# FFN heads of a four-layer fp32 trunk: one weight sum moved ahead of a side's low half, and down weights split behind the last gate

## Chip, core and metric

The kernel runs on one core of a Trainium2 chip. The metric is device time in microseconds (us), the median of several runs. Five engines work side by side, each through its own instructions in order: TensorE (PE in the profile; PEld is its loading of stationary operands), VectorE (DVE), ScalarE (ACT), GpSimd (POOL) and SyncE (SP). SP and POOL issue the DMA transfers here, each in the order of its queue.

## What is computed

A trunk of four layers on a sequence of 512 tokens with 1024 channels. Each layer has a mixer (an S5 state space model in layers 0 and 3, gated linear attention in layer 1, differential attention in layer 2) and a gated feed-forward network, each behind an RMS norm. The change is in the feed-forward networks alone:

```python
D_MODEL = 1024; SEQ = 512; DEPTH = 4; FFN_HIDDEN = 2816

def swiglu_ffn(h, w_gate_up, w_down):
    g, u = jnp.split(h @ w_gate_up, 2, axis=-1)
    return (jax.nn.silu(g) * u) @ w_down

for layer in range(DEPTH):
    h = rmsnorm(x, norm_mix[layer])
    x = x + mixer(h)                      # S5, GLA or differential attention
    h = rmsnorm(x, norm_ffn[layer])
    x = x + swiglu_ffn(h, w_gate_up[layer], w_down[layer])
return rmsnorm(x, norm_final)
```

All data are float32.

## The kernel before

**Arithmetic.** A float32 product is made of three PE matmuls: each operand is split into a high half (rounded, by a cast on ACT) and a low half (the rest, by a subtraction on DVE), and high by high, high by low and low by high are summed in PSUM. For weights this is `high` (L346, ACT) and `low` (L350, DVE) into a tile `whl` that holds both halves. There are five `whl` buffers in turn, and three staging buffers `wst` into which SP loads weights (L336); some weights have staging tiles of their own (`slot`, `lent`, `halves`, `gain`; loaded at L568). A transfer that adds into what has landed is issued by POOL (L571). A staging buffer is free for the next load when `low` has read it.

**Gate and up products.** The hidden width of 2816 is cut into 11 blocks of 256. A block's gate and up columns, and the two halves of the 1024 channels, make a two by two scheme with seven products in place of eight, for two halves of the tokens (the steps are called one to seven). Each product is 24 matmuls (`seven_product`, L535) of a *side* (the normed tokens or a sum of their quarters, split in halves: `side`, `sides`) with a weight or a sum of weights. In the order of a block: one, five, six, two, seven, three, four. Five takes weight "1" (two quarters summed by the transfers), six takes "1" again after weight "22" was added into it on DVE (`add("22")`, L628), four takes it once more after "21" was added (`add("21")`, L628). The results leave their PSUM banks by copies on ACT or sums on DVE (L607, L614, L625, L639, L645, L652). `scaled` multiplies a gate by the tokens' norm factor on DVE (L580) and applies Silu on ACT (L581). The products with up (L653, L662) are split again into high and low (L672 on ACT, L673 on DVE): this is `act`, the operand of the down product.

**Heads.** The first two blocks (a and b) of an FFN are interleaved by hand, in an order written as a string of steps (`plan`), because the sides and norm factors are made in the same stretch. `split21a` is `high` and `low` of weight "21" of block a; `highFa` and `lowFa` are `high` and `low` of its weight "1" after the second sum, for the product four. `high22` and `low22` split the *side* "22" (L218 on ACT, L223 on DVE), which only four reads. `add21a` and `add21b` are the second sums. FFN 2 has a plan of its own; FFN 0, 1 and 3 share the other.

**Down products.** When four blocks are done (then four more, then three; in FFN 0 three, three, three and two), their `act` tiles are multiplied with the down weights, in two halves of 512 output channels (`d` = 0 and 1): `gemm_b` takes a weight of two times 128 rows at a time (here called d0, d1, d2, ... in the order of their use), 24 matmuls each (L370, L371, L372 in turn), into four PSUM banks, which `add_x` adds to the residual on DVE (L518).

**Order of the work.** On PE, ACT, DVE and the queues a scheduler orders the instructions by the data they need and by their order in the program; `issue_after(x)` puts the instructions of its body behind x where they are on x's engine. So in the kernel before, the splits of the first down weights stand among the last steps of the block before them, as soon as a `whl` buffer is free. In FFN 0 and FFN 1 small *jobs* run beside the down products (`job`): in FFN 0 parts of the second S5 layer's set-up, in FFN 1 tables for the attention (`dtab`) and phase tables (`s5_phases`: four ACT instructions at L1213, sums on DVE at L1215 to L1221, sines on ACT at L1224 to L1226, then a POOL transfer at L1305). The tables of FFN 1 live in `whl` buffers too.

Of the kernel before, what the change touches and what calls it, by code (L numbers as in the profile page):

```python
# [15 lines left out]
AF = mybir.ActivationFunctionType  # L16
ALU = mybir.AluOpType
# [135 lines left out]
class Sides(Left):  # L153
# [66 lines left out]
    def low(self, name):  # L220
        for ks, y in self.of(name):
            o = self.place[name][:, :, ks]
            self.tr.nc.vector.tensor_tensor(o[:, 1], y, o[:, 0].bitcast(F32), op=ALU.subtract)  # L223
# [45 lines left out]
class Trunk:  # L269
    def __init__(self, ctx, tc, ins, out):  # L270
        self.ctx, self.tc, self.nc = ctx, tc, tc.nc
        self.i = ins
        self.out = out
        self.rot = self.edges = 0
        nc = self.nc
        ep = lambda name, bufs, **k: ctx.enter_context(tc.tile_pool(name=name, bufs=bufs, **k))
        self.cp = ep("const", 1)
        self.xp = ep("xp", 1)
        self.hp = ep("hp", 2)
        self.wp = ep("wp", 3)  # L280
        self.np_ = ep("normp", 2)
        self.sp = ep("small", 8)
        self.ps = ep("psum", 1, space=PSUM)
        self.dp = ep("dram", 1, space=DRAM)
        self.ident = self.cp.tile([P, P], F32, name="ident")
        make_identity(nc, self.ident)
        self.two_pi = float(np.nextafter(np.float32(TWO_PI), np.float32(0)))
        self.mhalf = self.cp.tile([P, 8], F32, name="mhalf")
        nc.vector.memset(self.mhalf[:], -0.5)
        self.ones = self.cp.tile([P, P], F32, name="ones")  # L290
        nc.gpsimd.memset(self.ones[:], 1.0)
        self.dq = nc.sync
        self.jobs = iter(())
        self.last = {}
        self.pend = []
        self.guard, self.lazy = None, False

    def edge(self, pool, n):

# [43 lines left out]

    def high(self, w, a, n):
        hl = self.wp.tile([P, 2, a, n], F32R, tag="whl", name="whl", bufs=5)
        self.last["high"] = self.nc.scalar.copy(hl[:, 0], w[:])  # L346
        return hl

    def low(self, hl, w):
        self.last["low"] = self.nc.vector.tensor_tensor(hl[:, 1], w[:], hl[:, 0].bitcast(F32), op=ALU.subtract)  # L350

    def job(self):
# [18 lines left out]
        mm(out, lh, rl, start=False, stop=False)  # L371
        self.last["mm"] = mm(out, ll, rh, start=False, stop=last)  # L372

    def gemm_b(self, stat, w, nk, c0, evac, k0=0, tail=0, between=(), ahead=None, jobs=False):

        between = iter(between)
        accs = [self.acc() for _ in range(NT)]
        hl = nxt = None  # L380
        for kb in range(0, nk - tail, 2):
            hl = nxt or self.wb(w, k0 + kb, c0)
            nxt = self.wb(w, k0 + kb + 2, c0) if jobs and kb + 2 < nk - tail else None
            if kb == 2:
                self.flush()
            for a in range(2):
                k = kb + a
                for t in range(NT):
                    self.mm3(
                        accs[t][:], stat(k, 0, t), stat(k, 1, t), hl[:, 0, a], hl[:, 1, a],  # L390
                        k == 0, k == nk - 1,
                    )
                    if k == nk - 1:
                        evac(t, accs[t])
                    if jobs:
                        self.job()
            next(between, lambda: None)()
        if tail:
            hls = [self.wb(w, k0 + kb, c0) for kb in range(nk - tail, nk, 2)]
            if ahead:  # L400
                self.hand_all()
                ahead()
            for t in range(NT):
                for j in range(tail):
                    k = nk - tail + j
                    self.mm3(
                        accs[t][:], stat(k, 0, t), stat(k, 1, t), hls[j // 2][:, 0, j % 2],
                        hls[j // 2][:, 1, j % 2], k == 0, k == nk - 1,
                    )
                evac(t, accs[t])  # L410
# [129 lines left out]
    def seven_block(self, fp, slots, left, wgu, b, turn, na):  # L540


        nc = self.nc
        v = nc.vector
# [32 lines left out]
        def scaled(out, src, th):  # L577
            R = left.R[:, th * 256 : (th + 1) * 256].unsqueeze(1).broadcast_to([P, 2, 256])
            g = lambda y: y.rearrange("p (j n) -> p j n", j=2)
            v.tensor_tensor(g(out[:]), g(src[:]), R, op=ALU.mult)  # L580
            nc.scalar.activation(out[:], out[:], AF.Silu)  # L581

        def direct():
            load("11", 0, 0)
# [96 lines left out]
    def ffn(self, l, left, after=None, turn=False, aside=None, small=None):  # L681


        jobs = bool(aside or small)
        i = self.i
        wgu, wd = i["ffn_w_gate_up"][l], i["ffn_w_down"][l]
        nxt = None
        r = left.r
        with self.tc.tile_pool(name=f"ffn{l}", bufs=1, reuse_waits="tile") as fp:
# [23 lines left out]
            if l == 2:  # L713
                plan = """
                    split21a one:a split21b square flush one:b total3 total1 one_out:a finish high1 low1 total2 split1a
                    high2 low2 one_out:b two:a two:b split1b high3 two_out:a five:a add22a highSa two_out:b lowSa
                    five_out:a five:b turn add22b highSb diag lowSb low3 split3a six:a spread five_out:b rows six:b
                    six_out:a split3b seven:a six_out:b total4 split22a high4 low4 seven:b seven_out:a split22b
                    high22 low22 three:a add21a highFa add21b lowFa highFb three:b lowFb seven_out:b gate1:a four:a gate1:b
                    four:b three_out:a three_out:b  # L720
                """
            else:
                plan = """
                    split21a one:a split21b square flush one:b total1 one_out:a finish high1 low1 total2 split1a high2 low2
                    one_out:b two:a two:b split1b high3 two_out:a five:a add22a highSa two_out:b lowSa five_out:a five:b
                    add22b highSb diag lowSb low3 split3a six:a spread five_out:b rows six:b six_out:a split3b seven:a
                    six_out:b total4 split22a high4 low4 seven:b seven_out:a split22b three:a seven_out:b gate1:a gate1:b
                    high22 low22 three:b add21a highFa add21b lowFa highFb lowFb four:a four:b three_out:a three_out:b
                """
            for step in plan.split():  # L730
                name, _, n = step.partition(":")
# [2 lines left out]
                elif name[-1] in "ab":  # L734
                    word = next(w for w in ("split", "add", "high", "low") if name.startswith(w))
                    w = name[len(word) : -1]
# [7 lines left out]
                elif name == "turn":  # L744
                    r = self.turn_x(left.r) if turn else r
# [12 lines left out]
            b0 = 0  # L758
            for nb in (4, 4, 3) if na == 4 else (3, 3, 3, 2):
                acts = []  # L760
                for n in range(b0, b0 + nb):
                    b = blocks[n]
# [12 lines left out]
                stat = lambda k, part, t: acts[k // 2][:, part, k % 2, t * P : (t + 1) * P]  # L775
                if b0 + nb == 11 and after is not None:
                    nxt = (Chunks if turn else Left)(self, after)
                for d in range(2):
                    tail = 4 if d == 1 and b0 + nb == 11 else 0
                    self.gemm_b(stat, wd, 2 * nb, d * 512, self.add_x(d, nxt, r), k0=2 * b0, tail=tail, jobs=jobs)  # L780
                b0 += nb
            for _ in self.jobs:
                pass
# [1642 lines left out]
```

## Time and profile before

| | |
|---|---|
| Median of 3 runs | 2325.21 us (2324.91 to 2325.57) |
| The profiled execution, its own time | 2320.61 us |
| Its span, first to last instruction | 2318.9 us |
| Mean granted TensorE clock | 0.989 |
| FFN 0, about 240 to 640 us: PE busy | 393.2 of 400.0 us |
| FFN 1, about 842 to 1120 us: PE busy | 272.1 of 278.0 us |
| FFN 2, about 1455 to 1800 us, with work of the next stage: PE busy | 338.9 of 345.0 us |
| FFN 3, about 1975 to 2312 us: PE busy | 327.7 of 337.0 us |

The profile is of one execution. Its parts used here: the page (busy time of each engine); the list of waits (who waited for whom, in total, how often, the longest); the timeline (instructions in order of time, equal ones that follow each other merged, with their start and duration and, in brackets, the idle time of the engine before them and what ended it); windows (busy time of each engine in a stretch, and the clock granted to PE). L numbers are lines of the kernel before; "q" behind an engine's name is its queue of transfers.

### The profile page before, as it was taken

The page shows a single profiled execution, that of the slowest core. Times are in us where ns is not written, and L with a number is a line of the kernel's source. Part 1 is how long each engine was busy: PE and PEld are TensorE (multiplying, and loading weights), DVE is VectorE, ACT ScalarE, POOL GpSimd, SP SyncE. Part 2 cuts the span into 40 slices and gives each one's busy share as a digit, 9 for nine tenths or more (in the row PEclk, how much of TensorE's full clock was granted, in tenths as well). Part 3 has the DMA queues.
Part 4 walks back from the last instruction along what each step waited for, and adds up shares of the span by engine and source line. Part 5 has one row for each costly group of instructions (what it writes and reads, how often), then busy time and mean ns, then how long its engine had stood idle before and what let it go on. Part 6 is the DMA issues. An engine that isn't in the chain of part 4 may idle for free. (4 is left out here: it accounts for less than half of the span.)

```text
span 2318.9 us, 37158 instructions
## 1 busy us (share of the span) xinstructions
PE 2221.3 (96%) x14847; PEld 1969.5 (85%) x14847; DVE 1593.3 (69%) x2461; ACT 1112.6 (48%) x1769; POOL 284.5 (12%) x394
## 2 busy tenths in 40 slices
PE   5899999999999999999999999999999899999997
PEld 3788979898877789898988887899999788989996
DVE  8784877786624578776744675976766965967674
ACT  5533645454453355555535675654534224635342
POOL 1000141522000010101002131110000100101000
PEclk8999999999999999999999999999999999999999
DMA  4156567663422457575336365876641555766531
GB/s 85 37 141 171 138 166 183 169 175 97 129 73 73 133 138 196 155 191 156 100 124 151 91 150 143 216 206 152 171 96 46 140 158 151 191 161 161 160 81 64
DMA packets 293927, 319.91 MB, mean 138 GB/s; under 512 B 70077, under 2 KB 233177, under 8 KB 293498
## 3 DMA queue, kind: packets, MB, share of 16 engines
q1 hardware_dynamic: 231130, 235.79, 33.9%
q0 software_dynamic: 62624, 81.75, 19.1%
q8 instruction: 117, 1.92, 0.3%
q14 instruction: 56, 0.46, 0.1%
HBM read 285.62 MB, written 16.65 MB: 130 GB/s over the span
## 5 line engine op out<-in xcount | busy, mean ns | idle before, releaser
L350 DVE TENSOR_TENSOR whl<-wst,whl 128x1024 fp32r<-128x1024 f32 x272 | 331.9, 1223 | 280.6 <-ACT whl L346 279.8
L346 ACT CAST whl<-wst 128x1024 fp32r<-128x1024 f32 x272 | 285.6, 1052 | 382.8 <-PE acc L372 259.8
L535 PE MATMUL a<-side,whl 128*128 128x256 f32 x3168 | 384.9, 278 | 10.0 <-ACT whl L346 5.9
L535 PEld LDWEIGHTS a<-side,whl 128*128 128x128 f32 x3168 | 371.7, 189 | 12.5 <-ACT whl L346 7.2
L370 PE MATMUL acc<-whl,act 128*128 128x512 f32 x704 | 278.0, 395 | 1.2 <-DVE g L580 0.8
L371 PE MATMUL acc<-whl,act 128*128 128x512 f32 x704 | 274.9, 391 | 0.0
L372 PE MATMUL acc<-whl,act 128*128 128x512 f32 x704 | 274.7, 390 | 0.0
L535 PE MATMUL c<-side,whl 128*128 128x256 f32 x2112 | 255.6, 277 | 5.8 <-DVE whl L350 5.8
L535 PEld LDWEIGHTS c<-side,whl 128*128 128x128 f32 x2112 | 248.1, 189 | 6.6 <-DVE whl L350 6.6
L350 DVE TENSOR_TENSOR whl<-slot,whl 128x1024 fp32r<-128x1024 f32 x105 | 127.9, 1223 | 65.7 <-ACT whl L346 65.1
L370 PEld LDWEIGHTS acc<-whl,act 128*128 128x128 f32 x704 | 132.1, 188 | 30.8 <-DVE g L580 1.2
L372 PEld LDWEIGHTS acc<-whl,act 128*128 128x128 f32 x704 | 132.2, 188 | 27.8
L371 PEld LDWEIGHTS acc<-whl,act 128*128 128x128 f32 x704 | 132.2, 188 | 26.0 <-issue 0.2
L346 ACT CAST whl<-slot 128x1024 fp32r<-128x1024 f32 x105 | 110.1, 1054 | 73.9 <-PE acc L372 28.1
L370 PE MATMUL acc<-whl,hT 128*128 128x512 f32 x352 | 142.9, 406 | 2.1 <-DVE ro L2151 1.5
L371 PE MATMUL acc<-whl,hT 128*128 128x512 f32 x352 | 137.9, 392 | 1.0 <-DVE whl L350 1.0
L372 PE MATMUL acc<-whl,hT 128*128 128x512 f32 x352 | 137.9, 392 | 0.0
L535 PE MATMUL a<-sides,whl 128*128 128x256 f32 x1056 | 134.0, 283 | 1.6 <-DVE x L518 1.6
L535 PE MATMUL d<-sides,whl 128*128 128x256 f32 x1056 | 133.4, 283 | 1.3 <-ACT whl L346 1.3
L535 PEld LDWEIGHTS a<-sides,whl 128*128 128x128 f32 x1056 | 129.5, 191 | 2.7 <-issue 2.0
L535 PEld LDWEIGHTS d<-sides,whl 128*128 128x128 f32 x1056 | 128.9, 191 | 1.9 <-ACT whl L346 1.9
L571 POOL DMA_DIRECT2D wst<-in_ffn_w_gate_up_dram x44 | 57.1, 1297 | 436.5 <-DMA wst<-in_ffn_w_gate_up_dram 239.1
(449 smaller groups left out, 3909.1 us busy)
## 6 DMA issues: line engine op xcount, KB each, us to landing
wst<-in_ffn_w_gate_up_dram SPq DMA_DIRECT2D x88, 512.0 KB, 4.7
wst<-in_ffn_w_down_dram SPq DMA_DIRECT2D x88, 512.0 KB, 4.5
slot<-in_ffn_w_gate_up_dram SPq DMA_DIRECT2D x69, 512.0 KB, 5.5
wst<-in_ffn_w_gate_up_dram POOLq DMA_DIRECT2D x44, 512.0 KB, 6.2
halves<-in_ffn_w_gate_up_dram SPq DMA_DIRECT2D x42, 512.0 KB, 5.7
wst<-in_s_w_glu_dram SPq DMA_DIRECT2D x32, 512.0 KB, 4.5
wst<-in_gla_w_in_dram SPq DMA_DIRECT2D x24, 512.0 KB, 3.7
wst<-in_diff_w_qkv_dram SPq DMA_DIRECT2D x24, 512.0 KB, 3.7
```

The costliest lines, as they stand in the source:

```text
L346: self.last["high"] = self.nc.scalar.copy(hl[:, 0], w[:])
L350: self.last["low"] = self.nc.vector.tensor_tensor(hl[:, 1], w[:], hl[:, 0].bitcast(F32), op=ALU.subtract)
L370: mm(out, lh, rh, start=first, stop=False)
L371: mm(out, lh, rl, start=False, stop=False)
L372: self.last["mm"] = mm(out, ll, rh, start=False, stop=last)
L535: mm(o, hl[:, x, k, c], side[:, y, k], start=first and not (j or k or n), stop=k == 3 and n == 2, skip_group_check=True,)
L571: nc.gpsimd.dma_start(w[:], left.quarter(*plus, b), accum_op=ALU.add)
```

## The change

Two edits. In the plan of FFN 0, 1 and 3 the step `add21a` stands ahead of `high22 low22`, not behind `three:b`. And `gemm_b` takes `behind`, a copy of the last instructions by name: while it is set, `high` issues its cast behind the last Silu on ACT and `low` its subtraction behind the last scaling on DVE. `ffn` gives it for the first half of the columns (`d` = 0) of every group in FFN 1, 2 and 3. The first weight of such a call (d0) is made before it is set. The number of instructions on each engine stays as it is.

```diff
@@ Trunk.__init__
+        self.behind = None
@@ high, low
         hl = self.wp.tile([P, 2, a, n], F32R, tag="whl", name="whl", bufs=5)
-        self.last["high"] = self.nc.scalar.copy(hl[:, 0], w[:])
+        with self.tc.issue_after(self.behind["silu"].ins) if self.behind else nullcontext():
+            self.last["high"] = self.nc.scalar.copy(hl[:, 0], w[:])
         return hl
 
     def low(self, hl, w):
+        with self.tc.issue_after(self.behind["scaled"].ins) if self.behind else nullcontext():
+            self.low_now(hl, w)
+
+    def low_now(self, hl, w):
         self.last["low"] = self.nc.vector.tensor_tensor(hl[:, 1], w[:], hl[:, 0].bitcast(F32), op=ALU.subtract)
@@ gemm_b
-    def gemm_b(self, stat, w, nk, c0, evac, k0=0, tail=0, between=(), ahead=None, jobs=False):
+    def gemm_b(self, stat, w, nk, c0, evac, k0=0, tail=0, between=(), ahead=None, jobs=False, behind=None):
...
             hl = nxt or self.wb(w, k0 + kb, c0)
+            self.behind = behind
             nxt = self.wb(w, k0 + kb + 2, c0) if jobs and kb + 2 < nk - tail else None
...
             next(between, lambda: None)()
+        self.behind = None
         if tail:
@@ scaled
-            v.tensor_tensor(g(out[:]), g(src[:]), R, op=ALU.mult)
-            nc.scalar.activation(out[:], out[:], AF.Silu)
+            self.last["scaled"] = v.tensor_tensor(g(out[:]), g(src[:]), R, op=ALU.mult)
+            self.last["silu"] = nc.scalar.activation(out[:], out[:], AF.Silu)
@@ ffn, the plan of FFN 0, 1 and 3
-                    high22 low22 three:b add21a highFa add21b lowFa highFb lowFb four:a four:b three_out:a three_out:b
+                    add21a high22 low22 three:b highFa add21b lowFa highFb lowFb four:a four:b three_out:a three_out:b
@@ ffn, the down products
-                    self.gemm_b(stat, wd, 2 * nb, d * 512, self.add_x(d, nxt, r), k0=2 * b0, tail=tail, jobs=jobs)
+                    self.gemm_b(stat, wd, 2 * nb, d * 512, self.add_x(d, nxt, r), k0=2 * b0, tail=tail, jobs=jobs,
+                                behind=None if d or l == 0 else dict(self.last))
```

In the built kernel the order on PE differs in one place (two small transposes of a job, L2037, stand one down product later), that on POOL not at all, that on SP in three places (in the heads of FFN 1 and 3, and for the job tables of FFN 1). On DVE and ACT the casts and low halves of d1, d2 and d3 stand behind the last scaling and Silu of each group of FFN 1, 2 and 3, and the jobs of FFN 1 are woven in differently.

## Prediction

> **What bounds the kernel now.** I read the page first, then TensorE's list of waits, then the timeline around each wait that the change can reach.
>
> ```profile
> span 2318.9 us, 37158 instructions
> PE 2221.3 (96%) x14847; PEld 1969.5 (85%) x14847; DVE 1593.3 (69%) x2461; ACT 1112.6 (48%) x1769; POOL 284.5 (12%) x394
> ```
>
> TensorE (PE) is busy for 96% of the span, so an edit on VectorE (DVE) and ScalarE (ACT) can only win time in which PE stands still for them. Its waits that have to do with FFN weights are few:
>
> ```profile
> PE a L535 <- ACT whl L346: 5.9, 3, 2.0
> PE c L535 <- DVE whl L350: 5.8, 3, 4.3
> PE a L535 <- DVE whl L350: 3.0, 4, 0.8
> PE a L535 <- DVE x L518: 1.6, 1, 1.6
> PE acc L370 <- DVE g L580: 0.8, 1, 0.8
> ```
>
> Columns: total us, times, longest. The first row has three equal waits, one in each of the heads of FFN 0, 1 and 3, whose plan is the one edited. The 4.3 us wait is in FFN 2, whose plan stays. The last row is the only wait for a gate, and it is in FFN 0, which the second edit leaves out. Here is the head of FFN 1 (start, duration, what ended the idle time before):
>
> ```profile
> 860.14 5.60 PE L535 MATMUL c<-side,whl 128*128 128x256 f32 x48
> 861.23 1.29 DVE L580 TENSOR_TENSOR r<-r,R 128x512 f32<-128x512 f32 x2
> 863.09 1.04 ACT L218 CAST side<-halves 128x1024 fp32r<-128x1024 f32 x1
> 864.16 1.23 DVE L223 TENSOR_TENSOR side<-halves,side 128x1024 fp32r<-128x1024 f32 x1 [1.64 <-ACT side L218]
> 865.30 2.35 DVE L628 TENSOR_TENSOR lent<-lent,slot 128x1024 f32<-128x1024 f32 x2
> 866.61 2.20 ACT L346 CAST whl<-lent 128x1024 fp32r<-128x1024 f32 x2 [2.48 <-DVE lent L628]
> 867.68 2.38 DVE L350 TENSOR_TENSOR whl<-lent,whl 128x1024 fp32r<-128x1024 f32 x2
> 867.70 0.50 PE L535 MATMUL a<-side,whl 128*128 128x256 f32 x2 [1.96 <-ACT whl L346]
> 868.96 5.69 PE L535 MATMUL a<-side,whl 128*128 128x256 f32 x46 [0.76 <-DVE whl L350]
> 877.12 1.23 DVE L350 TENSOR_TENSOR whl<-halves,whl 128x1024 fp32r<-128x1024 f32 x1
> 878.40 2.79 PE L535 MATMUL c<-side,whl 128*128 128x256 f32 x22 [0.63 <-DVE whl L350]
> 882.17 0.50 PE L535 MATMUL d<-sides,whl 128*128 128x256 f32 x2 [0.45 <-ACT whl L346]
> ```
>
> and DVE's busy time in a window of it (window, length, busy, granted clock, DMA share, GB/s):
>
> ```profile
> 867.68:878.35 10.67, 10.67 (x15) 1.00 1.13 291
> ```
>
> DVE stands idle for 1.64 us while ACT casts the side's high half (L218), then does low22 (L223), the second sums of both blocks (L628 twice), and the low halves (L350 twice). PE has run out of work at 865.74 (860.14 + 5.60), makes two matmuls when the first high half is there, and goes on at 868.96 when the first low half is. From there DVE has no free moment until 878.35 (10.67 of 10.67 us), and PE's next stall, at 878.40, is for DVE again.
>
> **Part 1: add21a ahead of high22 and low22.** Nothing is added; one L628 moves into the hole. Step by step: the gate scalings end at 862.52 (861.23 + 1.29); add21a then takes some 1.2 us (half of 2.35) and ends by 863.7. Its operands are long there, since both were split and used in products before. Low22 still starts at 864.16, because it waits for L218. The steps behind it each stand one step earlier. DVE starts follow each other by 1.14 us (864.16 to 865.30), so add21b starts at 865.30 and lowFa at 866.44. HighFa needs only add21a and its turn behind L218: 864.1 to 865.2, ahead of PE. LowFa ends at 867.66, and PE's third matmul starts at about 867.73 in place of 868.96: 1.23 us. LowFb is nearer: add21b ends at 866.52, highFb runs 866.6 to 867.65, lowFb starts at 867.70, where it started 1.14 after 867.68, at 868.82 (the row holds two). That is 1.12 us, and since DVE is full from there to the stall at 878.40, PE's gain at that stall is 1.12, not 1.23. So 1.12 us for a head: FFN 0 and FFN 1.
>
> In FFN 3 the same stall has a second price:
>
> ```profile
> 2000.16:2003.57 3.41, 0.83 (x5) 0.43 (x4) 3.38 (x3) 2.10 (x3) 0.00 (x0) 1.00 1.11 338
> 2003.57:2006.98 3.41, 3.26 (x15) 3.27 (x16) 3.41 (x5) 1.90 (x2) 1.28 (x1) 0.50 1.10 350
> 273.02:276.43 3.41, 1.59 (x15) 1.39 (x13) 3.41 (x3) 0.96 (x1) 0.00 (x0) 1.00 0.65 207
> 277.82 5.50 PE L535 MATMUL a<-side,whl 128*128 128x256 f32 x46 [0.76 <-DVE whl L350]
> 2003.72 7.14 PE L535 MATMUL a<-side,whl 128*128 128x256 f32 x46 [0.76 <-DVE whl L350]
> 2008.07 0.69 DVE L580 TENSOR_TENSOR g<-a,R 128x512 f32<-128x512 f32 x1 [0.31 <-PE a L535]
> 2017.33 0.50 PE L535 MATMUL d<-sides,whl 128*128 128x256 f32 x2 [0.44 <-ACT whl L346]
> ```
>
> (Windows: length, busy PE, PEld, DVE, ACT and POOL, granted clock, DMA share and GB/s.) PE was busy for 0.83 of 3.41 us, and in the next 3.41 us its clock was 0.50; the 46 matmuls took 7.14 us, not 5.69 as in FFN 1. Behind a window with 1.59 us of work (FFN 0) the 46 took 5.50: no drop. After the change the hole is one of 1.78 us (two matmuls from 865.45 or so to 865.95, then nothing to 867.73), so any window keeps 3.41 - 1.78 = 1.63 us of work or more, and I expect the full clock. The 1.45 us are not all won, since DVE paces what follows: PE's stall of 882.17 lies 13.21 us behind 868.96, its twin at 2017.33 lies 13.61 behind 2003.72. The drop costs 0.40 in the end, DVE's own wait of 0.31 for PE among it. FFN 3: 1.12 + 0.40 = 1.52.
>
> The heads give 1.12 + 1.12 + 1.52 = 3.76 us.
>
> The Trainium skill ("TensorE: Matmul & The Clock Gate", Part 1: The HAM clock gate) has the clock halve after at least one idle window of about 3.4 us. Here no window of that head is wholly idle and the clock fell behind one with 0.83 us of work, so the measurement is the stricter and decides; by the rule the drop would have another cause and stay, and the heads would give 3.36.
>
> **Part 2: down weights behind the last gate.** In FFN 1, 2 and 3, at each of nine group ends, weights d1, d2 (and d3) of the first column half are now split behind the gate's scaling (DVE) and Silu (ACT); d0 is not. The cost is nothing as long as PE's work on d0 (5.46 us, from 2050.42 to 2055.88) hides it. FFN 3, first group:
>
> ```profile
> 2049.70 1.22 DVE L350 TENSOR_TENSOR whl<-wst,whl 128x1024 fp32r<-128x1024 f32 x1 [0.39 <-ACT whl L346]
> 2051.45 0.68 DVE L580 TENSOR_TENSOR g<-a,R 128x512 f32<-128x512 f32 x1
> 2052.83 0.63 ACT L581 ACTIVATE g<-g 128x512 f32<-128x512 f32 x1
> 2050.42 0.39 PE L370 MATMUL acc<-whl,act 128*128 128x512 f32 x1
> 2055.88 0.39 PE L370 MATMUL acc<-whl,act 128*128 128x512 f32 x1
> 2042.45 12.13 SPq L336 DMA_DIRECT2D wst<-in_ffn_w_down_dram  x5
> 2058.46 16.69 SPq L336 DMA_DIRECT2D wst<-in_ffn_w_gate_up_dram  x4
> 2093.95 2.31 PE L535 MATMUL a<-sides,whl 128*128 128x256 f32 x18
> ```
>
> PE starts on d0 at 2050.42 and on d1 at 2055.88. With the scaling no earlier than now: it ends at 2052.13, Silu at about 2052.8, d1's cast (1.05, as L218) at 2053.9, its low half (1.23) at 2055.2. That leaves 0.7 us, and about 1.4 when the scaling moves up, since L350 at 2049.70 no longer stands before it. Then the gate's last product, the act halves and d2 follow, 5.4 us of PE apart. Bounds: 0 as long as these hold, a loss of the excess where they do not. A gain is excluded in FFN 2 and 3, because PE has no wait there for a gate or an act. Each low half also hands back a staging buffer, so d4's load, one of the five from 2042.45 on, now waits for 2055.2, at most 13 us longer, and SP's queue behind it with it: d5 to d7 and the four gate/up loads of the next block (from 2058.46). Those belong to products from 2093.95 on, 19 us behind the last issue (2058.46 + 16.69), so I price it at 0.
>
> FFN 1 is different, because small jobs (the phase tables, L1213 to L1226) share DVE, ACT and the whl buffers there, and the built order moves them:
>
> ```profile
> 942.94 1.65 ACT L1213 ACTIVATE phases<-mrow,magic,s5f 128x128 f32<-128x128 f32 x4 [3.62 <-DMA cs<-phases]
> 955.70 1.05 ACT L346 CAST whl<-wst 128x1024 fp32r<-128x1024 f32 x1 [1.53 <-DMA cs<-phases]
> 954.20 0.43 DVE L1215 TENSOR_SCALAR phases<-phases 128x512 f32<-128x512 f32 x1 [3.38 <-ACT phases L1213]
> 960.66 2.72 DVE L518 SCALAR_TENSOR_TENSOR x<-acc,rcol,x 128x512 f32<-128x512 f32 x4
> 961.55 3.10 PE L535 MATMUL a<-sides,whl 128*128 128x256 f32 x24 [1.57 <-DVE x L518]
> ```
>
> PE loses 1.57 us at 961.55 because L518, which empties its bank, stands on DVE behind a late phase table. In the new order of ACT, table A's last sine comes behind table B's four L1213 (1.65 us, as at 942.94) and a weight's cast (1.05), which partly fill holes: some 2 us later. B's three sines follow each other, no longer mixed with table C's L1213, and come some 1.7 us earlier; the wait of 3.62 us at 942.94 is for B's buffer. Followed through the two DMA waits, the cast at 955.70 and L518 come about 1 us earlier. Bounds: the whole stall won (+1.57), or A's 2 us carried to the end (-2.0). I take +0.9, near the followed chain.
>
> Sum: 3.76 + 0.9 = 4.66 us of the profiled execution's 2320.61 us, which is 4.60 us below the median of the runs (2325.21). Taken off the median: 2320.55, written 2320.6.
>
> **The rivals.**
> - *The heads alone.* The jobs of FFN 1 land where they were or a little later. For it: their chain has two DMA waits whose lengths I do not control. 2325.21 - 3.76 = 2321.4, with the 2 us carried through 2323.4.
> - *The gain is given back in the next blocks.* The window 867.68 to 878.35 has a DMA share of 1.13: transfers are queued full, and PE ahead by 1.1 us could meet weights that have not landed. Against it: DVE and ACT show no wait for a DMA there. If FFN 0, 1 and 3 each keep a third, 1.3 us: 2323.9.
> - *The clock drop of FFN 3 stays*, because its cause is not PE's idle time: 0.40 less, 2321.0. Against it: the row with 0.83 us of work, and FFN 0's without a drop. The rule of the Trainium skill named above is what speaks for it.
> - *Slower: d1 is late at all nine group ends.* If Silu or the cast is held up by one act pair (ACT's cast and DVE's low half of a 128x512 tile, near 0.65 each as L581 and L580) twice over, d1 comes 2.6 us later, 1.2 to 1.9 past the margin; nine times 1.2 is 10.8 us, less 4.66: 2331.3. It decides from 1.4 us of delay on, and outweighs all gains above 1.9 us. Against it: in the built order d1's low half stands right behind the gate's product (L662), ahead of the last act half (L673).
>
> **How the numbers follow.** Forecast, the heads with part or all of the FFN 1 stall: 0.58. Heads alone: 0.22. Given back: 0.08. The drop stays: 0.05. Slower: 0.07. What a measurement of this kernel can tell from no change is about 0.2%, 4.65 us, so the line is at 2320.56, where the forecast stands. Of its 0.58 I put 0.42 beyond the line, for its largest unknown reaches further up from the line (the whole stall: 5.3 us) than down. Faster 0.42; within 0.2%, all the rest but the last: 0.51; slower 0.07. The range takes in the heads alone and the gain given back above (2323.9 and the 1.3 us left in it), and below the whole stall (2319.9) with one or two drops less of 1.45 us in other stages, whose windows all shift: 2317.0 to 2325.2.
>
> **What would show it.** In the heads, one L628 ahead of L223 in the hole, PE's waits for ACT L346 gone, and one wait for DVE L350 of about 1.8 us in their place; no clock of 0.50 in FFN 3's head; the stalls like 878.40 still there. At group ends, no wait of L370 or L371 for L346 or L350. In FFN 1, the wait for L518 near 0.6 us. A wait of 1 us or more for d1, or new waits for a DMA in the blocks behind a head, would make the prediction wrong.

## The result, and the profile after

| | before | after |
|---|---|---|
| Median | 2325.57 us (2324.91 to 2326.74, 5 runs) | 2316.13 us (2311.62 to 2318.8, 5 runs) |
| Ratio, 95% interval | | 0.995 (0.9936 to 0.9963) |
| Profiled execution, its own time; span | 2320.61; 2318.9 us | 2316.13; 2314.4 us |

The kernel became 9.4 us faster, twice the 4.66 us forecast, and lies just below the range. The page of the changed kernel gives the span and TensorE's (PE's) busy time:

```profile
span 2314.4 us, 37179 instructions
PE 2219.4 (96%) x14847; PEld 1970.1 (85%) x14847; DVE 1593.2 (69%) x2461; ACT 1108.2 (48%) x1769; POOL 284.6 (12%) x394
```

PE is busy for 1.9 us less with the same 14847 matmuls, so less than half of the 4.5 us between the two profiled spans is matmul time; the rest is waiting that ended. (The two medians lie 9.4 us apart: the profiled execution of before was a fast one.) PE's list of waits (total us, times, longest); the lines have new numbers: L543 was L535, L348 was L346, L356 was L350, L376 was L370, L588 was L580, L526 was L518, and below L661 was L653 and L680 was L672:

```profile
PE c L543 <- DVE whl L356: 7.2, 4, 4.3
PE a L543 <- DVE whl L356: 6.0, 4, 1.7
PE acc L376 <- DVE g L588: 2.6, 1, 2.6
PE d L543 <- ACT whl L348: 1.3, 3, 0.4
PE a L543 <- DVE x L526: 1.2, 1, 1.2
```

The row of 5.9 us in three waits for ACT's cast is gone. In its place the row for DVE's low half grew from 3.0 to 6.0 us, its longest from 0.8 to 1.7. The row for c grew from 5.8 us in three waits to 7.2 in four. The wait for a gate, which neither edit touches in FFN 0, grew from 0.8 to 2.6. The head of FFN 1, timeline (start, duration, idle time before and what ended it):

```profile
859.90 1.22 DVE L636 TENSOR_TENSOR lent<-lent,slot 128x1024 f32<-128x1024 f32 x1
860.55 1.04 ACT L218 CAST side<-halves 128x1024 fp32r<-128x1024 f32 x1
861.62 1.23 DVE L223 TENSOR_TENSOR side<-halves,side 128x1024 fp32r<-128x1024 f32 x1 [0.50 <-ACT side L218]
862.76 1.22 DVE L636 TENSOR_TENSOR lent<-lent,slot 128x1024 f32<-128x1024 f32 x1
863.05 0.39 PE L543 MATMUL a<-side,whl 128*128 128x256 f32 x2
863.90 2.50 DVE L356 TENSOR_TENSOR whl<-lent,whl 128x1024 fp32r<-128x1024 f32 x2
865.17 5.50 PE L543 MATMUL a<-side,whl 128*128 128x256 f32 x46 [1.73 <-DVE whl L356]
```

The first sum (L636, before L628) now fills DVE's hole, of which 0.50 us is left. PE makes two matmuls at 863.05 without a wait and then waits once, 1.73 us. Windows around it (length, busy PE, PEld, DVE, ACT and POOL with counts, granted clock, DMA share, GB/s):

```profile
861.81:865.22 3.41, 1.68 (x16) 1.49 (x14) 3.36 (x4) 1.85 (x3) 0.76 (x1) 1.00 1.18 241
865.22:868.63 3.41, 3.41 (x30) 3.41 (x31) 3.41 (x4) 1.82 (x2) 0.52 (x1) 1.00 1.10 359
```

PE works 1.68 us of the emptiest window, and the next one has the full clock.

### The profile page after: what moved, and what is told of

Same layout as the page of the kernel before. It is cut to its first block, busy times and chain, and to the rows that moved or that the text cites. A ratio compares the mean times of both kernels' runs of the same rounds, so it can differ in the third digit from the quotient of the medians.

```text
span 2314.4 us, 37179 instructions
## 1 busy us (share of the span) xinstructions
PE 2219.4 (96%) x14847; PEld 1970.1 (85%) x14847; DVE 1593.2 (69%) x2461; ACT 1108.2 (48%) x1769; POOL 284.6 (12%) x394
## 5 line engine op out<-in xcount | busy, mean ns | idle before, releaser
L356 DVE TENSOR_TENSOR whl<-wst,whl 128x1024 fp32r<-128x1024 f32 x272 | 331.1, 1222 | 264.5 <-ACT whl L348 263.4
L348 ACT CAST whl<-wst 128x1024 fp32r<-128x1024 f32 x272 | 284.3, 1050 | 336.9 <-PE acc L378 232.8
L543 PE MATMUL a<-side,whl 128*128 128x256 f32 x3168 | 382.4, 277 | 6.1 <-DVE whl L356 6.0
L543 PEld LDWEIGHTS a<-side,whl 128*128 128x128 f32 x3168 | 369.9, 188 | 7.8 <-DVE whl L356 6.7
L376 PE MATMUL acc<-whl,act 128*128 128x512 f32 x704 | 278.0, 395 | 2.6 <-DVE g L588 2.6
L543 PE MATMUL c<-side,whl 128*128 128x256 f32 x2112 | 256.2, 278 | 7.2 <-DVE whl L356 7.2
L543 PEld LDWEIGHTS c<-side,whl 128*128 128x128 f32 x2112 | 248.4, 189 | 8.2 <-DVE whl L356 8.2
L356 DVE TENSOR_TENSOR whl<-slot,whl 128x1024 fp32r<-128x1024 f32 x105 | 127.8, 1222 | 66.0 <-ACT whl L348 65.9
L376 PEld LDWEIGHTS acc<-whl,act 128*128 128x128 f32 x704 | 132.1, 188 | 31.9 <-DVE g L588 3.0
L348 ACT CAST whl<-slot 128x1024 fp32r<-128x1024 f32 x105 | 110.0, 1053 | 74.0 <-PE acc L378 28.2
L376 PE MATMUL acc<-whl,hT 128*128 128x512 f32 x352 | 142.8, 406 | 2.1 <-DVE ro L2160 1.5
L543 PE MATMUL a<-sides,whl 128*128 128x256 f32 x1056 | 133.9, 283 | 1.2 <-DVE x L526 1.2
L543 PE MATMUL d<-sides,whl 128*128 128x256 f32 x1056 | 133.4, 282 | 1.3 <-ACT whl L348 1.3
L543 PEld LDWEIGHTS a<-sides,whl 128*128 128x128 f32 x1056 | 129.4, 191 | 2.3 <-issue 1.6
L543 PEld LDWEIGHTS d<-sides,whl 128*128 128x128 f32 x1056 | 128.8, 191 | 1.9 <-ACT whl L348 1.9
L680 ACT CAST act<-r 128x512 fp32r<-128x512 f32 (+1 forms) x110 | 66.2, 644 | 105.1 <-DVE r L661 86.1
```

Of the source, the lines that this page charges most:

```text
L376: mm(out, lh, rh, start=first, stop=False)
L543: mm(o, hl[:, x, k, c], side[:, y, k], start=first and not (j or k or n), stop=k == 3 and n == 2, skip_group_check=True,)
L680: self.last["act high"] = nc.scalar.copy(dst[:, 0, j], src[:, j])
```

## The experiments

Eleven kernels, in three groups (e1 to e4, e5 to e8, e9 to e11), each group beside fresh runs of the kernel before. Times are medians, the ratio is to the kernel before of the same group.

| Label | us | kernel before | ratio, 95% interval |
|---|---|---|---|
| e1_before_again | 2324.79 | 2325.18 | 0.9998 (0.9987 to 1.0009) |
| e2_after_again | 2316.58 | 2325.18 | 0.9965 (0.9953 to 0.9977) |
| e3_plan_alone | 2317.84 | 2325.18 | 0.9967 (0.9956 to 0.9979) |
| e4_behind_alone | 2322.45 | 2325.18 | 0.999 (0.9978 to 1.0002) |
| e5_fill_heads | 2323.85 | 2325.61 | 0.999 (0.9977 to 1.0004) |
| e6_late_before | 2326.92 | 2325.61 | 1.0005 (0.9992 to 1.0017) |
| e7_late_behind | 2324.42 | 2325.61 | 0.9996 (0.9985 to 1.0007) |
| e8_fill_after | 2313.91 | 2325.61 | 0.9958 (0.9944 to 0.9971) |
| e9_behind_all | 2322.96 | 2327.04 | 0.9984 (0.9972 to 0.9996) |
| e10_behind_late | 2318.9 | 2327.04 | 0.9965 (0.9953 to 0.9977) |
| e11_behind_one | 2317.9 | 2327.04 | 0.9966 (0.9955 to 0.9977) |

One interval is some 2.5 us to each side, so the times part the two edits but not their pieces. The pieces come from the profiles. All kernels issue the same matmuls in the same order, but for small ones of the jobs in FFN 0 and 1 (e5's filler left out; e8 shown only up to its own, at 1496.81 us), so a stage can be measured in each profile from the start of one PE instruction to that of another. The stages below are those that start, in the profile of before, at 256.08, 860.03 and 1994.09 us (heads, to 297.04, 890.10 and 2025.05), 925.14 (to 966.10: the wait for L518 in FFN 1), and 1536.02 and 2050.08 (to 1800.08 and 2200.21: group ends of FFN 2 and 3). In brackets: windows of half clock in that head.

| Profile | FFN 0 | FFN 1 | FFN 3 | L518 | FFN 2 | FFN 3 ends |
|---|---|---|---|---|---|---|
| before | 40.95 | 30.07 | 30.96 (1) | 40.95 | 264.06 | 150.13 |
| e1 | 40.85 | 30.06 | 30.85 (1) | 43.27 | 265.01 | 150.16 |
| e4 | 40.95 | 31.25 (2) | 30.97 (1) | *39.50* | *264.12* | *150.13* |
| e6 | 42.27 (2) | 29.95 | 31.00 (1) | 40.94 | 265.45 | 150.13 |
| e7 | 42.32 (2) | 31.35 (2) | 31.11 (1) | *39.16* | *264.12* | *150.13* |
| e5, filler | 40.86 | 29.97 | 30.63 | 39.87 | 264.92 | 150.13 |
| e3 | *39.73* | *28.84* | *29.40* | 40.59 | 264.97 | 151.08 |
| after | *39.73* | *28.83* | *29.39* | *40.58* | *264.08* | *150.13* |
| e2 | *39.73* | *28.83* | *29.39* | *40.31* | *264.12* | *150.13* |
| e8 | *39.81* | *28.93* | | *39.91* | | |
| e9 | *39.72* | *28.81* | *29.38* | *39.94* | *264.08* | *150.13* |
| e10 | *39.73* | *28.83* | *29.39* | 41.84 | *264.12* | *150.13* |
| e11 | *39.73* | *28.81* | *29.41* | *40.01* | 264.67 | 150.13 |

In italics: stages that run in the new order.

### The two edits apart

e1 and e2 are the two kernels as they are. e3 is the kernel before with the new plan only:

```diff
-                    high22 low22 three:b add21a highFa add21b lowFa highFb lowFb four:a four:b three_out:a three_out:b
+                    add21a high22 low22 three:b highFa add21b lowFa highFb lowFb four:a four:b three_out:a three_out:b
```

and e4 the changed kernel with the old plan, so with `behind` alone.

> The kernel before, unchanged, profiled once more. Theory A (the saving is made of PE waits that a profile shows, and the first profiled execution of before, 2320.6 us, was a fast one of its kind): median 2325 to 2326 us; this profile shows, beside the three waits of about 1.96 us in the heads, some 4 to 5 us more of PE waits or half-clock stretches than the first one, in places that the first one did not have. Theory B (the profiled execution differs from the timed ones by something outside PE's waits, so the saving cannot be read in a profile): 2325 to 2326 us again, and the profile shows 2320 to 2321 us with the same waits.

> The changed kernel, profiled once more. Theory A: 2312 to 2319 us, median near 2316; the spread of 7 us comes from places where PE's clock drops or a transfer lands late, and the profile shows which. In the heads one wait of 1.73 us each, as in the first profile. Theory B: the same times, and nothing in the waits that differs between executions by more than 1 us.

> Only the plan edit (add21a ahead of high22 low22). My sum gives 1.12 + 1.12 + 1.52 = 3.8 us less than before: 2321.8 us. Rival (the heads give little, the saving is of the down weights): 2324 to 2326 us. Rival (the heads give all of the 9.4 us, by clock drops that the shorter hole avoids): 2316 us.

> Only the down weights behind the last gate, with the plan of before. My sum gives 0.9 us less than before, all of it at FFN 1's wait for L518: 2324.7 us. Rival (the saving beyond the heads, 9.4 - 3.8 = 5.6 us, is made here): 2320 us. Rival (the splits behind the gate cost, and the heads pay for it): above 2326 us.

The plan alone is worth 7.3 us (interval 4.9 to 10.2), `behind` alone 2.7 (from 5.1 gained to 0.5 lost). So by the medians both parts exceed the 3.76 and 0.9 us of the prediction; only for the plan does the interval leave out what was predicted. The second run of the kernel before is as slow as the first, and its profile, of an execution near the median, has what e1's theory A expected: a wait for L518 of 2.4 us in place of 1.6 with a window of half clock behind it (962.30 to 965.71), a wait for g of 0.6 us in FFN 2 that the first profile didn't have, and no more than the first in the heads. The table says where the rest is: a head of the old plan comes with and without windows of half clock, and the group ends of FFN 2 come at 264.1 and near 265.

What makes a late group end shows in FFN 3 of e3, whose weights are split in the old order. Timeline rows of ACT, DVE and PE:

```profile
2046.95 1.05 ACT L346 CAST whl<-wst 128x1024 fp32r<-128x1024 f32 x1 [3.50 <-DMA wst<-in_ffn_w_down_dram]
2048.04 1.23 DVE L350 TENSOR_TENSOR whl<-wst,whl 128x1024 fp32r<-128x1024 f32 x1 [1.49 <-ACT whl L346]
2049.18 0.68 DVE L673 TENSOR_TENSOR act<-r,act 128x512 fp32r<-128x512 f32 x1
2049.78 0.68 DVE L580 TENSOR_TENSOR g<-a,R 128x512 f32<-128x512 f32 x1
2050.52 0.50 PE L370 MATMUL acc<-whl,act 128*128 128x512 f32 x1 [0.66 <-DVE g L580]
```

and of the changed kernel at the same place:

```profile
2044.95 0.62 ACT L680 CAST act<-r 128x512 fp32r<-128x512 f32 x1 [4.90 <-DVE r L661]
2045.95 0.39 PE L376 MATMUL acc<-whl,act 128*128 128x512 f32 x1
2046.21 0.68 DVE L588 TENSOR_TENSOR g<-a,R 128x512 f32<-128x512 f32 x1
2048.59 1.23 DVE L356 TENSOR_TENSOR whl<-wst,whl 128x1024 fp32r<-128x1024 f32 x1 [0.25 <-ACT whl L348]
```

In e3 the transfer of d1 lands late. ACT stands at its cast for 3.50 us; DVE stands at its low half, 1.49 us of them with nothing else to do; behind that low half, on the same engine, stands the gate's scaling, which empties the bank that PE needs after its first nine matmuls on d0 (from 2047.65). PE waits 0.66 us, held up by weights that it doesn't need yet. In the changed kernel the scaling starts 0.26 us after PE began on d0, and no cast or low half that waits for a transfer stands ahead of it.

One stall is one case; the other profiles bear it out. Six of them have the old order in FFN 2 and 3, each with six group ends. PE waits for g at exactly seven of the 36, those where ACT had waited 2.60 us or more for d1 to land (2.60, 2.68, 2.71, 2.76, 2.85, 2.93 and 3.50), and its wait grows with ACT's (0.25, 0.33, 0.36, 0.39, 0.50, 0.58 and 0.66). At the other 29 ACT waited 2.50 us at most. In the new order ACT doesn't wait for d1 at any group end of FFN 2 and 3, and PE never for g.

One gain of `behind` is outside the table. FFN 1 from 890.10 to 925.14 us takes 35.02 to 35.05 us in the six profiles without `behind` in FFN 1 and 34.55 to 34.59 in the seven with it. PE waits for no engine there. It is the one place where the order on PE differs: in before the two transposes L2037 stand at 919.75 and 920.33, each followed by a matmul that starts late, and in the changed kernel both stand together at 916.46. That is 0.45 us, which the prediction doesn't have.

### Filler in the heads

e5 is the kernel before, with matmuls in the hole of the three heads whose result nobody reads:

```diff
-                    ... highFb lowFb four:a four:b three_out:a three_out:b
+                    ... highFb lowFb fill four:a four:b three_out:a three_out:b
+                elif name == "fill":
+                    side = left.place["4"]
+                    for o in (self.sbank("fill"), self.sbank("fill")):
+                        for _ in range(6):
+                            self.nc.tensor.matmul(o[:, :256], side[:, 0, 0, :P], side[:, 0, 0], start=True, stop=True)
```

> The kernel before, with twelve matmuls of 128x256 (0.107 us each, 1.28 us in all) that nobody reads, issued into the 1.96 us hole ahead of product four:a in the heads of FFN 0, 1 and 3. The order and every wait of the real work stay as before. Theory A (clock): in the old head PE works only about 1.2 to 1.6 us in some 3.41 us window around its two waits, and whether the clock falls to 0.50 in the next window depends on where the free-running windows lie; counted over all positions of the windows in the two profiles of before, the chance is 0.47 (bound at 1.4 us of work) to 0.70 (bound at 1.55 us) for each head. With the filler no window holds less than 2.4 us of work: no clock of 0.50 in any of the three heads, the mean granted clock over all executions up from 0.985 to about 0.986 to 0.987, and the time down by 3 x 0.5 to 0.7 windows x 0.9 to 1.7 us = 1.3 to 3.6 us: 2321.6 to 2323.9. Theory B (the plan alone gained 7.3 us by the waits alone, or by something outside the heads): no change, 2325.2 within 0.8, and the clock as before.

Windows of FFN 1's head in e7, which has the old plan without filler:

```profile
866.95:870.36 3.41, 1.45 (x12) 1.13 (x10) 3.38 (x4) 1.41 (x2) 1.28 (x1) 1.00 1.16 251
870.36:873.77 3.41, 2.65 (x13) 2.57 (x13) 3.41 (x4) 2.58 (x3) 0.00 (x0) 0.50 1.15 292
873.77:877.18 3.41, 3.41 (x18) 3.41 (x18) 2.35 (x5) 0.78 (x2) 0.00 (x0) 0.50 1.13 294
```

the same of FFN 3's head in e1:

```profile
2006.78:2010.19 3.41, 1.62 (x11) 1.43 (x12) 3.38 (x4) 3.30 (x4) 0.69 (x1) 1.00 1.10 360
2010.19:2013.60 3.41, 3.41 (x18) 3.41 (x17) 3.28 (x5) 1.24 (x2) 0.59 (x1) 0.50 1.12 325
```

and FFN 1's head in e5, first PE's timeline, then windows:

```profile
866.14 1.60 PE L746 MATMUL fill<-side 128*128 128x256 f32 x12
868.26 0.50 PE L535 MATMUL a<-side,whl 128*128 128x256 f32 x2 [0.52 <-ACT whl L346]
869.53 1.68 PE L535 MATMUL a<-side,whl 128*128 128x256 f32 x12 [0.76 <-DVE whl L350]
```

```profile
865.32:868.74 3.42, 2.90 (x23) 2.51 (x21) 3.39 (x4) 1.47 (x2) 0.00 (x0) 1.00 1.12 303
868.74:872.15 3.41, 2.65 (x23) 2.63 (x23) 3.41 (x4) 2.53 (x3) 1.28 (x1) 1.00 1.09 357
```

Behind a window with 1.45 or 1.62 us of work the clock fell to 0.50; in e7 the first slow window held a stall itself (2.65 us of work), and the next was slow too. With filler the real matmuls still wait (the first for what the filler leaves, the third for 0.76 us), so they don't start sooner, and no head has a slow window. Of the 15 heads of the old plan without filler 9 have one or two, 13 slow windows in all (all five heads of FFN 3, four of the ten others); of the 21 heads of the new plan none, and none of the three with filler. Nine in 15 is 0.60, inside the chance of 0.47 to 0.70 that e5's expectation worked out. The mean granted clock over the timed executions rose from 0.9844 (27 of before) to 0.9878 (11 of e5); e3 has 0.9890. The time fell by 1.8 us, inside the expected 1.3 to 3.6, though by itself its interval (5.3 gained to 0.9 lost) doesn't part it from none; the clock and the windows do.

### A later transfer

e6 loads the second down weight (d1) of a group's first column half twice into its tile, in FFN 1 to 3; e7 does so with `behind`:

```diff
-        self.nc.sync.dma_start(w[:], src)
+        for _ in range(2 if self.late else 1):
+            self.nc.sync.dma_start(w[:], src)
```

> The kernel before, with the second of the down weights that each group of FFN 1, 2 and 3 uses for its first column half loaded twice into the same tile, so that it lands later by one more load (some 2 to 4 us). Theory A (in-order queues): ACT waits at its head for the landing to cast this weight, DVE behind it for the cast, and the gate's product on DVE (L580) and the Silu stand behind those; so at the group ends PE waits for g at the first L370 after the cut-off, at most of the ten group ends of FFN 1 to 3 (in the profiles of before: 1 of them or none), 1 to 3 us each, and the kernel is slower than before by 10 to 30 us. Rival (the waits for the gate have another cause, such as a bank or the previous block): few waits for g, the waits are for whl (the weight itself), and the time is the same as that of the twin with the gate ahead of the split.

> The same doubled load, with the part of the change that splits these weights behind the last gate (and the old plan of the heads). Theory A: no wait of PE for g at the group ends of FFN 1 to 3; what remains are waits for the late weight itself (whl), so the kernel is faster than the twin without it by the waits for g, 5 to 20 us. Rival: as slow as the twin within 2 us.

The doubled load did not do what it was meant to. ACT's longest wait for d1 at the group ends of e6 is 2.71 us, within the 3.50 that the other profiles of the old order have, so d1 landed no later than in them. (FFN 1 to 3 have nine group ends, not ten.) e6 is 1.3 us above the kernel before, not 10 to 30, and has two waits for g in FFN 2 (0.36 and 0.33 us). e7 has none and is 2.5 us faster than its twin, but e4 differs from before by as much without any doubled load. As a test the pair decides nothing; what speaks for theory A is the list of 36 group ends above.

### `behind` in other FFNs

e9 sets it in FFN 0 too, e10 in FFN 2 and 3 only, e11 in FFN 1 only (all with the new plan):

```diff
-                                behind=None if d or l == 0 else dict(self.last))
+                                behind=None if d else dict(self.last))            # e9
+                                behind=None if d or l < 2 else dict(self.last))   # e10
+                                behind=None if d or l != 1 else dict(self.last))  # e11
```

> The changed kernel with the split behind the last gate in FFN 0 too, which the change leaves out. In FFN 0 PE waits at its first group end for g by DVE (L580 of before) in every profile taken of a kernel with the old order there but one: 0.76, 1.08, 1.07, 0.84, 2.56, 1.39, 1.07, 1.23 and 2.10 us, and ACT's cast of a down weight has waited 4.4 to 5.2 us for its landing just before, DVE's low half 2.9 to 3.7 us for that cast, ahead of the gate's product. Theory A (the late landing holds ACT, then DVE, and so the gate): this wait of PE for g is gone, and nothing over 0.5 us for whl takes its place; the time falls by about the wait, 0.8 to 1.8 us, under 2316.4. Rival (the gate is late for another reason, the block before it): the wait stays above 0.7 us or turns into one for the down weight of the same size, and the time stays at 2316.4.

> The changed kernel without the split behind the gate in FFN 1 (kept in FFN 2 and 3). Theory A (two halves of what the second part gains: waits for the gate at group ends of FFN 2 and 3, about 1 us an execution, and the wait for L518 in FFN 1, about 1 us): no wait for g in FFN 2 and 3, but the wait for L518 near 960 us back at 1.2 to 2.4 us; 2317.0 to 2318.0. Rival (all of it is the waits for the gate): the wait for L518 under 1 us as in the changed kernel's profiles (0.92 and 1.18), 2316.4.

> The changed kernel with the split behind the gate in FFN 1 alone. Theory A: the wait for L518 stays under 1.2 us, and at one or two group ends of FFN 2 and 3 PE waits 0.4 to 0.7 us for g again, each with 0.3 us more around it; 2317.0 to 2318.0. Rival (all of it is FFN 1's wait for L518): no wait for g in FFN 2 and 3, 2316.4.

FFN 0 in the changed kernel, where its order is the old one; timeline of ACT and DVE ahead of the 2.6 us wait for the gate:

```profile
303.63 1.05 ACT L348 CAST whl<-wst 128x1024 fp32r<-128x1024 f32 x1 [5.18 <-DMA wst<-in_ffn_w_down_dram]
304.71 1.23 DVE L356 TENSOR_TENSOR whl<-wst,whl 128x1024 fp32r<-128x1024 f32 x1 [3.68 <-ACT whl L348]
305.86 0.68 DVE L588 TENSOR_TENSOR g<-a,R 128x512 f32<-128x512 f32 x1
```

PE's waits in e9, for the small jobs of FFN 0 (after: 1.3 us for L1200):

```profile
PE xps L1200 <- DVE halves L1054: 4.1, 1, 4.1
PE rps L1154 <- DVE halves L1052: 1.2, 1, 1.2
```

and its windows there:

```profile
328.91:332.32 3.41, 0.19 (x6) 0.22 (x8) 2.10 (x4) 0.00 (x0) 2.64 (x4) 1.00 0.39 82
332.32:335.73 3.41, 3.41 (x22) 2.75 (x20) 3.12 (x10) 1.61 (x6) 2.27 (x5) 0.50 0.99 166
```

In e9 PE waits nowhere for g, as theory A said, but the time went the other way: 4.1 us under the kernel before, where e2 is 8.6 and, in e9's own group, e10 8.1 and e11 9.1 under it. The 1.0 to 2.6 us won at the group end came back as 4.1 us of waiting for a small job (L1054, DVE) and a window of half clock behind it, then 1.2 us for another: FFN 0 from 297.04 to 614.23 us takes 322.74 us in e9 and 317.19 to 319.45 in the other twelve profiles. The mechanism was right and the next thing late was not foreseen. PE's waits in e10:

```profile
PE a L543 <- DVE x L526: 2.4, 1, 2.4
PE acc L376 <- DVE g L588: 2.3, 1, 2.3
PE acc L376 <- DVE x L526: 0.6, 1, 0.6
```

and in e11:

```profile
PE acc L376 <- DVE g L588: 1.2, 2, 1.0
PE a L543 <- DVE x L526: 0.6, 1, 0.6
```

e10 has no wait for g outside FFN 0 (the 2.3), and the wait of L518's kind is back in FFN 1, twice: theory A. In e11 that wait is 0.6, and the second wait for g, 0.2 us, is the only one in FFN 2 and 3: less than theory A's one or two of 0.4 to 0.7. Both times lie within the interval of the changed kernel.

### Filler in the changed kernel

e8 repeats idle matmuls in three holes of PE outside the change: 26 times the first matmul of a product in FFN 2, 16 transposes and twice 10 matmuls between FFN 2 and the last S5 layer:

```diff
+        for _ in range(fill):
+            mm(bank[:, :256], hl[:, 0, 0, :P], side[:, 0, 0], start=True, stop=True)
...
+        for _ in range(16):
+            nc.tensor.transpose(p[:, 0], tr.ident[:], tr.ident[:])
...
+            for _ in range(10 if left and kk == 0 else 0):
+                mm(yb[:, 0], U[:, bs(0)], mop[:, bs(0)], start=True, stop=True)
```

> The changed kernel, with matmuls that change nothing (the first matmul of a product repeated ahead of itself, or a transpose into a bank that the next one overwrites) in three other holes of PE: 26 of 0.107 us in the 4.3 us hole of FFN 2's head, 16 transposes in the 2.55 us hole and 10 matmuls in the 3.05 us hole between FFN 2 and the last S5 layer. Theory A (clock by work in a window): the one window of 0.50 behind the first and the two behind each of the others go, 4 to 5 windows of 1.7 us at most, of which part is covered by later waits: 3 to 8 us off 2316.4, and the mean granted clock from 0.987 to about 0.989. Theory B (the clock falls by something else than PE's idle time): 2316.4 within 1.5.

Windows at FFN 2's stall in the changed kernel, then in e8:

```profile
1500.09:1503.51 3.42, 0.55 (x4) 0.55 (x5) 3.42 (x7) 1.33 (x3) 0.00 (x0) 1.00 1.14 289
1503.51:1506.92 3.41, 3.41 (x18) 3.41 (x17) 2.30 (x3) 1.04 (x1) 0.00 (x0) 0.50 1.18 238
```

```profile
1498.84:1502.25 3.41, 1.94 (x17) 1.75 (x16) 3.41 (x6) 1.15 (x3) 0.00 (x0) 1.00 1.14 305
1502.25:1505.67 3.42, 2.74 (x22) 2.33 (x20) 2.31 (x3) 1.87 (x2) 0.00 (x0) 1.00 1.17 238
```

The slow windows behind all three holes are gone, and the mean granted clock over its timed executions is 0.9908, against 0.9872 for e2. The median is the lowest of all, 2313.91, but 2.7 us under e2's (3.1 by what each gains on its kernel before) is the low end of the expected 3 to 8 or just below it, and the intervals overlap. What the five slow windows that are gone could give beyond that may be waited for elsewhere; this was not followed. It is the fastest kernel run here, by a margin that these runs don't establish.

## Why the prediction was wrong

**The heads' waits** were right: predicted 3 x 1.12 = 3.36 us, measured from e5 (no slow windows on either side) to the new plan 40.86 + 29.97 + 30.63 - (39.73 + 28.83 + 29.39) = 3.5. So were the signs named for the heads: one L636 ahead of L223, the waits for ACT gone, one wait of 1.73 us (1.8 predicted), 1.68 us of work in the emptiest window (1.63 predicted), no half clock in FFN 3's head.

**The clock term was mis-sized**, and this is the first failed step: "The drop costs 0.40 in the end", counted once, in the head where the one profile had it. The size was about right for one slow window in FFN 3 (30.96 against e5's 30.63). But the same hole stands in all three heads, and whether a window of 3.41 us catches too little work is a matter of where it starts. Over five profiles, 9 heads of 15 were hit, and FFN 0 and 1 pay more, 1.3 to 1.5 us, when they are hit. The sum of the three heads is 102.98 us on the mean of these five (101.98, 101.76, 103.17, 103.22, 104.78), and e5's is 101.46: 1.5 us an execution in place of 0.40, give or take some 0.5 by the scatter of five. Heads in all: 102.98 - 97.95 = 5.0 us, not 3.76. The prediction knew that the windows shift: it put "one or two drops less of 1.45 us in other stages" into its range, but not into its sum. The rival by which the drop stays is out: filler alone took it away. The Trainium skill ("TensorE: Matmul & The Clock Gate", Part 1: The HAM clock gate) has the clock halve after at least one window that is idle throughout; that is too narrow for what the runs show, since it also fell behind windows with 1.45 and 1.62 us of work. In the table the same hole is hit in one execution and spared in the next, and the grid on which the slow windows lie starts elsewhere in each profile (last section). The traces agree there with the same section of the Trainium skill, which has the windows run free of the program.

**"A gain is excluded in FFN 2 and 3, because PE has no wait there for a gate or an act"** is the second failed step. That PE did not wait there was true of one execution. In the old order FFN 2 takes 264.85 us on the mean of six profiles (264.06 to 265.45), and in the new one 264.11 on the mean of six (264.08 to 264.12); FFN 3's group ends have 150.29 against 150.13. That is 0.9 us. The seven waits for g, of 0.25 to 0.66 us, stand in the profiles of the old order, none in those of the new.

**FFN 1's stall** was predicted at +0.9 us; the stage has a mean of 41.24 in the old order (before, e1, e3, e5, e6, e10) and 39.92 in the new (seven profiles): 1.3 us, or 0.9 without e1, whose stall has a window of half clock behind it. The sign and size held on the mean. For one execution the size was luck: the wait itself varies, 0.5 to 2.4 us in the old order, none to 1.2 in the new, and where about 0.6 was predicted the profile after has 1.2. The 0.45 us of the two transposes come on top; the prediction priced the order on PE at nothing without a word. e10, which has the old order in FFN 1 alone, has the stall back at 2.4 us and the two transposes apart, so both gains belong to FFN 1's own `behind`. How the small jobs' transfers set it was followed only by argument.

**The costs priced at nothing** were nothing: no wait of PE for d1 at a group end of FFN 1 to 3. In the changed kernel's FFN 3, d1's low half ends at 2049.82 (2048.59 + 1.23) and PE comes to it at 2051.41 (2045.95 + the 5.46 of d0), 1.6 us later; 1.4 was predicted. The slower rival and the one by which the gain is given back to transfers are out.

**The sum** from the profiles: 5.0 + 0.9 + 1.3 + 0.45 = 7.7 us. For `behind` alone that is 2.65 against 2.7 by the times, for the plan 5.0 against 7.3 (interval 4.9 to 10.2). For both the times show 8.6 (e2; interval 5.3 to 10.9) and 9.4 (the ratio's interval is 8.6 to 14.9, which 7.7 misses). What makes the remaining 1 to 2 us stays open; that windows fall otherwise in the stages behind a head that is shorter may be in it, but this was not tried. The profiles can't settle it: the stretch ahead of the first head, which no edit touches, alone takes 252.9 to 258.3 us in them.

Behind both failed steps stands one choice: the sum was made on a single profiled execution that ran 4.6 us under the median. About half of that gap is what this execution happened not to have: against the means of the old order it was spared 1.0 us in the heads, 0.9 at the group ends of FFN 2 and 3 and 0.3 at FFN 1's stall.

## What to carry to other kernels

When the profiled execution is well below the median, ask which stalls it was spared; a hole that may cost a slow window costs it in some share of executions, and every hole of that shape counts, not only the one that was hit. On an engine that works in order, an instruction that waits for a transfer should stand behind those whose results another engine needs sooner, even where today's profile shows no wait. Before taking a stall away, look at what is due next: e9 removed one of 2 us and met one of 4.

## What the runs showed of the hardware

In the heads the clock fell to half behind 3.41 us windows in which PE worked for 1.45 and 1.62 us, and not behind one with 1.59 (FFN 0 before) or 1.68 (after), so the boundary lies near 1.6 us there and isn't sharp in these records. It is no rule for other places. In the changed kernel the clock also fell behind a window with 1.73 us of work (1414.76 to 1418.17, ahead of FFN 2). And in twelve of the thirteen profiles it fell near 675 us, behind a row like this one of before:

```profile
672.45 3.77 PE L1881 MATMUL dps<-ind,la 128*128 128x2 f32 x32
```

By the profile PE is busy for all of the window 672.37 to 675.78, and the clock granted in the next one is 0.50. These matmuls are two columns wide. So busy time alone doesn't decide.

Matmuls whose result nobody reads keep the clock up: no slow window in e5's three heads, none behind e8's three holes. In a slow window less idle time is enough for another: 2.65 us of work in 3.41 at half clock were followed by a second slow window (e7, 870.36), and 2.65 at full clock were not (e5, 868.74). Over the profiles, between 130 and 2300 us, a slow window with up to 2.88 us of work had another behind it (e9, 1817.12), and one with 2.96 us or more had none (before, 1505.22).

In each profile the slow windows lie on one grid: in before those that start at 1505.22, 1805.60 and 2003.57 are 88 and 146 times 3.4133 us from the first. Against the program's own work the grid lies elsewhere in each profile: the first slow window at FFN 2's stall of 4.3 us starts 2.37 us ahead of the end of that stall in e5 and 0.85 us behind it in e10. So one execution pays for a hole that the next one is spared.
